# A mixture-of-experts layer: gathering tokens already transposed, in a fixed TensorE order, from weights stored tile by tile

## The chip, the core and the metric

The kernel runs on one core of one Trainium2 chip. The metric is the device time of one execution in microseconds (us). TensorE is called PE in the profile, its weight loads PEld, VectorE DVE, ScalarE ACT, GpSimd POOL and SyncE SP. SP issues nearly all transfers from HBM; its queue is written SPq.

## What is computed

One layer on 256 tokens of 2048 float32 features. Its first part is a token mixer (stick-breaking attention, a state-space layer, an mLSTM, three gated projections and an output projection), which reads most of the other float32 weights. Its second part, which most of this text is about, is a mixture of 32 experts:

```python
gates = (one_hot(g_idx, N_GROUPS)[:, :, None] * within[:, None, :]).reshape(-1, N_EXPERTS)
hid = silu(einsum('td,edf->tef', t, w1)) * einsum('td,edf->tef', t, w3)
y = einsum('tef,efd->td', hid * gates[:, :, None], w2)
```

Each token goes to one of 4 groups and there to 2 of 8 experts. An expert has `w1` and `w3` (2048 x 256 each) and `w2` (256 x 2048): 6 MiB, and 192 MiB (201.3 MB) for all 32. All are read once.

## The kernel before, in words

**The mixer.** Weight matrices are read in tiles of 512 rows by 512 columns (`load_raw`, DMA on L118) into a ring of three 1 MiB buffers. Each tile is split into a high and a low part (`split`: ACT cast on L131, DVE subtraction on L132), and three matmuls are made of it (L142 to L144). A tile is a 512-column piece of 512 rows, so its source runs are 2 KiB long. The conditioning matrix `w_ada` is read the same way: its first tiles by `ada_pe` (DMA L321, matmul L327) and `ada_first` (L295), in 2 KiB runs, the rest by `ada_rest` (L353 on DVE), in 4 KiB runs. Nothing of the mixer can start before the 8 MiB of `ada_pe` are there, as they give the modulation of the first input block.

**The router.** After the output projection a chain of small DVE operations finds for each token its experts and its place (rank) among the tokens of each expert pair. `keep_warm` matmuls fill PE meanwhile. In this part the order of PE, DVE and ACT is written out by hand (`manual_schedule`).

**The experts.** Experts are taken in 8 units of four; a unit is two half-groups of 64 tokens, and two `Pair` steps (`n`, with `el` = 0 and 1) of two experts each. A unit's tokens are gathered by matmul with a 0/1 selection (`sel_unit`, L1276). `Gather.rows` (L1312) has the selection as stationary operand and gives tokens on partitions; `scale` (L1317, ACT) multiplies by the norm; `turn` transposes on PE (L259, tile `xgT`) so that features are on partitions; `finish` modulates into `XG` (`modulate`, L1284 on ACT, L1287 on DVE). The transposes read every fourth column. The gather of unit u+1 is spread over the two pairs of unit u.

A `Pair` loads 12 tiles of 1 MiB (`load_in`, L1377: `w1` and `w3` for four row blocks and two experts, each tile as two DMAs of 512 KiB in 4 KiB runs; `load_out`, L1391: `w2`, four DMAs of 1 MiB in 8 KiB runs; in the very last pair L1388, 4 KiB runs). The tiles go round 11 buffers (`moe_raw`). `mm_in` multiplies `XG` by `w1` and `w3` (tile `h`), `hidden` applies the gated activation (ACT L1409, DVE L1410), `hidden_turn` transposes it (tile `hT`, copied on L1419), `mm_out` multiplies by `w2` (tile `y`). Both run on L1397, as two half-array matmuls, one per expert, at column positions 0 and 64:

```python
for h in range(2):
    sl = slice(64 * h, 64 * h + 64)
    nc.tensor.matmul(o[sl, :], lhsT=lhsT[:, sl], rhs=rhs(h), start=start, stop=stop,
                     tile_position=(0, 64 * h), skip_group_check=True)
```

At the end of a unit its four 512-column results are scaled and split (L1431, L1432, L1436), and in the next unit they are scattered back to the tokens by matmul and addition (`combine_mm`, tile `sc`, L1446; `combine_add`, L1455). Between router and last pair the order of the instructions on each engine is the framework's, not the program's. After the last pair come the final norm (L1722 to L1724) and the output (L1717).

Of the kernel before, what the change touches and what calls it, by code (L numbers as in the profile page):

```python
# [10 lines left out]
F32 = mybir.dt.float32  # L11
# [33 lines left out]
def kernel(ctx: ExitStack, tc: tile.TileContext, A, out, dbg=None):  # L45
# [44 lines left out]
    def cols4(v):  # L90
        return v.rearrange("(j p k) -> p j k", p=P, k=4)

    craw = cp.tile([P, 4, 4], F32, name="craw")
    nc.sync.dma_start(out=craw, in_=cols4(A["c"]))
    x_load()
    nc.gpsimd.dma_start(out=cst[:, :256], in_=A["consts"][:, :256])
    ball = cp.tile([P, 24, 4], F32, name="ball")
    nc.gpsimd.dma_start(out=ball[:, :8], in_=cols4(A["b_ada"])[:, :8])
    gmix = cp.tile([P, 4, 4], F32, name="gmix")
    nc.gpsimd.dma_start(out=gmix, in_=cols4(A["norm_mix_g"]))  # L100
    gmoe = cp.tile([P, 4, 4], F32, name="gmoe")
# [150 lines left out]
    def rows4(mat, c0):  # L252
        return lambda j: mat[512 * j:512 * j + 512, c0:c0 + 512].rearrange("(p k) c -> p k c", k=4)

    def rows_kp(mat, c0):
        return lambda j: mat[512 * j:512 * j + 512, c0:c0 + 512].rearrange("(k p) c -> p k c", p=P)
# [52 lines left out]
    def ada_pe(j):  # L309
# [6 lines left out]
        for jr in range(4):  # L316
            for kp in range(2):
                raw = pap.tile([P, 2, 2, 512], F32, tag="raw", bufs=3, name=f"ada{j}_{jr}_{kp}")
                for v in range(2):
                    c0 = v * D + 512 * j  # L320
                    nc.sync.dma_start(out=raw[:, v], in_=A["w_ada"][512 * jr:512 * jr + 512, c0:c0 + 512]  # L321
                                      .rearrange("(p k) c -> p k c", k=4)[:, 2 * kp:2 * kp + 2, :])
# [14 lines left out]
    def ada_rest():  # L337
        cols = []
        for v in (2, 3, 4, 5):
            for half in range(2):  # L340
                acc = pbp.tile([P, 1024], F32, tag="acc", bufs=1, name=f"accr{v}_{half}")
                for n in range(16):
                    jr, kp, q = n // 4, n // 2 % 2, n % 2
                    if q == 0:
                        c0 = v * D + 1024 * half
                        raw = load_raw(A["w_ada"][512 * jr:512 * jr + 512, c0:c0 + 1024]
                                       .rearrange("(p k) c -> p k c", k=4)[:, 2 * kp:2 * kp + 2, :],
                                       (2, 1024), f"adar{v}_{half}_{jr}_{kp}")
# [60 lines left out]
    def s5_params():  # L409
# [115 lines left out]
        nc.gpsimd.dma_start(out=br, in_=A["s5_b_re"].rearrange("(j g) p h -> (g p) j h", g=2))  # L525
        nc.gpsimd.dma_start(out=bi, in_=A["s5_b_im"].rearrange("(j g) p h -> (g p) j h", g=2))
# [42 lines left out]
        for r, nm in enumerate(("s5_c_re", "s5_c_im")):  # L569
            cc = cut(0, 8, 64)  # L570
            nc.gpsimd.dma_start(out=cc, in_=A[nm].rearrange("(u g) h p -> (g h) u p", g=8))
# [174 lines left out]
    def gates_chunk():  # L746
        wif = pap.tile([P, 2, 2, 512], F32, tag="raw", bufs=3, name="wif")[:, 0, 0, :128].rearrange("p (k c) -> p k c", k=16)
        for j in range(4):
            nc.gpsimd.dma_start(out=wif[:, 4 * j:4 * j + 4, :],
                                in_=A["w_in"][512 * j:512 * j + 512, COL["gates"]:COL["gates"] + 8]  # L750
                                .rearrange("(p k) c -> p k c", k=4))
# [199 lines left out]
    for j in range(4):  # L951
# [12 lines left out]
        if j == 2:  # L964
            nc.sync.dma_start(out=cst[:, 256:], in_=A["consts"][:, 256:])
            nc.sync.dma_start(out=ball[:, 8:], in_=cols4(A["b_ada"])[:, 8:])
            nc.sync.dma_start(out=gmoe, in_=cols4(A["norm_moe_g"]))
# [197 lines left out]
    wrg = pd.tile([P, 2, 16, 36], F32, tag="wrg", name="wrg")  # L1165
    wr, wg = wrg[:, 0], wrg[:, 1]
# [14 lines left out]
    L2 = pd.tile([P, 36], F32, name="L2")  # L1181
# [12 lines left out]
    L1 = pd.tile([P, 2, 36], F32, name="L1")  # L1194
# [22 lines left out]
    def out_copy(c4, tt, pt):  # L1217
        xt = pd.tile([P, 4, 128], F32, tag="x1T", bufs=2, name=f"x1Ts{c4}{tt}")
# [13 lines left out]
    def split_x1(tt, c4, part):  # L1232
        sl = slice(512 * c4, 512 * c4 + 512)
        if part == 0:
# [411 lines left out]
    for n in range(2 * NU - 1):  # L1646
# [24 lines left out]
        elif gat:  # L1671
            nxt.turn(2 * el)
# [108 lines left out]
```

## Time and profile before

| what | us |
|---|---|
| three runs of the kernel: lowest, median, highest | 1597.33, 1601.37, 1603.70 |
| the profiled execution, its own time | 1600.31 |
| its span in the trace | 1598.5 |
| PE busy | 1509.0 (94%) |
| DVE busy | 1015.1 (64%) |
| ACT busy | 568.6 (36%) |
| weights of the experts multiplied, first to last (PE) | about 1093 to 1580 |

Bytes moved: 488.13 MB, 201.3 MB of them weights of the experts. A row of the stretches view has, after the stretch and its length, the busy time and the number of instructions of PE, PEld, DVE, ACT and POOL, then the clock granted to PE (1.00 is 2.4 GHz), the mean busy share of the 16 DMA engines (overlapping packets can bring it a little over 1) and the GB/s that they moved. A row of the chain has start, length and what ran. In the groups view, a row gives line, engine, operation, tiles, shapes and count, then busy time and the mean of one in ns, then the idle time ahead of it.

### The profile page before, as it was taken

The numbers are of one execution on the slowest core, as the hardware profiler recorded it, in microseconds if no ns is written. First come the engines' busy times: TensorE is split into PE (matmuls) and PEld (weight loads), VectorE is DVE, ScalarE is ACT, GpSimd is POOL, SyncE is SP. The second block draws the span as 40 slices with busy tenths as digits, with TensorE's granted clock in tenths as the row PEclk, the third lists the DMA queues.
The fourth block names the chain that finished last, engine by engine and source line by source line (L and its number), as shares of the span: only waits on it lengthen the run. The fifth ranks groups of instructions, "written<-read, shape, count | busy, mean of one in ns | idle before, by whom it ended". The sixth has DMA issues, their size and how long they took to land.

```text
span 1598.5 us, 25021 instructions
## 1 busy us (share of the span) xinstructions
PE 1509.0 (94%) x10228; PEld 1140.2 (71%) x10228; DVE 1015.1 (64%) x1733; ACT 568.6 (36%) x755; POOL 39.0 (2%) x63
## 2 busy tenths in 40 slices
PE   4999999989999998999999999999999999999996
PEld 2999999888888988899999998874334433443332
DVE  0879997889879999999778866553213212222124
ACT  3554363774534333333444344342112111111112
POOL 1000010010000000000000010000000000000000
PEclk9999999999999999999999999999999999999998
DMA  9998967677787676777789976566999999999994
GB/s 343 386 348 305 319 191 222 220 223 261 247 300 265 229 264 231 273 264 264 263 308 327 318 267 241 207 228 257 414 413 412 413 402 374 412 392 411 404 412 183
DMA packets 172249, 488.13 MB, mean 305 GB/s; under 512 B 13876, under 2 KB 14048, under 8 KB 162784
## 3 DMA queue, kind: packets, MB, share of 16 engines
q1 hardware_dynamic: 168464, 473.27, 80.5%
q0 software_dynamic: 3088, 12.14, 2.3%
q8 instruction: 82, 1.34, 0.3%
q10 hardware_dynamic: 576, 1.05, 0.2%
q14 instruction: 39, 0.32, 0.1%
HBM read 479.06 MB, written 6.31 MB: 304 GB/s over the span
## 4 chain that ended last, share of the span: by engine, by line
PE 54%; DVE 25%; DMA 10%; issue 6%; ACT 4%; POOL 0%; SPq 0%; ACTq 0%; DVEq 0%; POOLq 0%
PE h L1397 14%; PE y L1397 9%; DVE accr L353 5%; DMA adar<-in_w_ada_dram 4%; DVE g_sb_w L132 2%; DVE g_ml_w L132 2%; PE sc L1446 2%; PE wo_b L143 2%; PE wo_b L144 2%; PE wo_b L142 2%; DVE bu L698 2%; PE xg L1312 2%; DVE s5pp L695 2%; DVE bu L697 1%; DVE s5qq L696 1%
## 5 line engine op out<-in xcount | busy, mean ns | idle before, releaser
L1397 PE MATMUL h<-w,XG 128*64 128x512 f32 x1024 | 245.3, 599 | 0.0
L1397 PEld LDWEIGHTS h<-w,XG 128*64 128x64 f32 x1024 | 75.7, 137 | 139.1 <-issue 137.4
L353 DVE SCALAR_TENSOR_TENSOR accr<-adar,ccol,accr 128x1024 f32<-128x1024 f32 x120 | 153.5, 1280 | 18.2 <-DMA adar<-in_w_ada_dram 17.3
L1397 PE MATMUL y<-w,hh 128*64 128x512 f32 x512 | 150.4, 598 | 0.5 <-ACT hh L1419 0.5
L1410 DVE SCALAR_TENSOR_TENSOR s<-h,gg,s 128x256 f32<-128x256 f32 x16 | 7.7, 484 | 167.8 <-ACT s L1409 167.8
L1455 DVE TENSOR_TENSOR x<-x,sc 128x512 f32<-128x512 f32 x64 | 43.0, 682 | 105.7 <-PE sc L1446 105.7
L1397 PEld LDWEIGHTS y<-w,hh 128*64 128x64 f32 x512 | 49.0, 136 | 81.5 <-issue 77.7
L1409 ACT ACTIVATE s<-h 128x256 f32<-128x256 f32 x16 | 6.1, 383 | 212.3 <-PE h L1397 212.3
L144 PE MATMUL g_sb_b<-hT,g_sb_w 128*128 128x256 f32 x256 | 73.1, 285 | 8.5 <-DVE g_sb_w L132 8.4
L144 PE MATMUL g_ml_b<-hT,g_ml_w 128*128 128x256 f32 x256 | 72.4, 283 | 3.3 <-DVE g_ml_w L132 3.3
L1287 DVE TENSOR_SCALAR XG<-xgT,G,modc 128x128 f32<-128x128 f32 x64 | 26.0, 410 | 77.0 <-ACT XG L1284 77.0
L144 PE MATMUL g_s_b<-hT,g_s_w 128*128 128x256 f32 x256 | 72.1, 282 | 1.6 <-DVE g_s_w L132 1.4
L142 PE MATMUL g_ml_b<-hT,g_ml_w 128*128 128x256 f32 x256 | 72.4, 283 | 0.0
L142 PE MATMUL g_sb_b<-hT,g_sb_w 128*128 128x256 f32 x256 | 71.9, 281 | 0.0
L142 PE MATMUL g_s_b<-hT,g_s_w 128*128 128x256 f32 x256 | 71.7, 280 | 0.0
L143 PE MATMUL g_s_b<-hT,g_s_w 128*128 128x256 f32 x256 | 71.6, 280 | 0.0
L143 PE MATMUL g_ml_b<-hT,g_ml_w 128*128 128x256 f32 x256 | 71.5, 279 | 0.0
L143 PE MATMUL g_sb_b<-hT,g_sb_w 128*128 128x256 f32 x256 | 71.4, 279 | 0.0
L132 DVE TENSOR_TENSOR wo_w<-wo_w,wo_w 128x1024 fp32r<-128x1024 f32 x32 | 39.0, 1223 | 31.8 <-ACT wo_w L131 31.6
L303 DVE SCALAR_TENSOR_TENSOR acc<-ada,ccol,acc 128x1024 f32<-128x1024 f32 x45 | 57.6, 1281 | 0.5
L131 ACT CAST g_ml_w<-g_ml_w 128x1024 fp32r<-128x1024 f32 x32 | 32.0, 1048 | 70.4 <-DMA g_ml_w<-in_w_in_dram 47.4
L144 PEld LDWEIGHTS g_sb_b<-hT,g_sb_w 128*128 128x128 f32 x256 | 48.1, 188 | 11.2 <-DVE g_sb_w L132 11.1
(506 smaller groups left out, 4361.7 us busy)
## 6 DMA issues: line engine op xcount, KB each, us to landing
w<-in_moe_w_dram SPq DMA_DIRECT2D x256, 512.0 KB, 9.2
adar<-in_w_ada_dram SPq DMA_DIRECT2D x64, 1024.0 KB, 5.5
w<-in_moe_w_dram SPq DMA_DIRECT2D x64, 1024.0 KB, 9.9
ada<-in_w_ada_dram SPq DMA_DIRECT2D x64, 512.0 KB, 7.5
g_sb_w<-in_w_in_dram SPq DMA_DIRECT2D x16, 1024.0 KB, 5.4
g_ml_w<-in_w_in_dram SPq DMA_DIRECT2D x16, 1024.0 KB, 5.4
g_s_w<-in_w_in_dram SPq DMA_DIRECT2D x16, 1024.0 KB, 6.1
wo_w<-in_w_out_dram SPq DMA_DIRECT2D x16, 1024.0 KB, 5.1
```

Of the source, the lines that this page charges most:

```text
L131: nc.scalar.copy(out=hv, in_=src)
L132: nc.vector.tensor_tensor(out=lv, in0=src, in1=hv.bitcast(F32), op=ALU.subtract)
L142: nc.tensor.matmul(o, lhsT=lhs[0], rhs=rhs[0], start=start, stop=False, **kw)
L143: nc.tensor.matmul(o, lhsT=lhs[0], rhs=rhs[1], start=False, stop=False, **kw)
L144: nc.tensor.matmul(o, lhsT=lhs[1], rhs=rhs[0], start=False, stop=stop, **kw)
L303: nc.vector.scalar_tensor_tensor(acc, raw[:, :, q], cs, acc, op0=ALU.mult, op1=ALU.add)
L353: nc.vector.scalar_tensor_tensor(acc, raw[:, q], cs, acc, op0=ALU.mult, op1=ALU.add)
L695: V.tensor_tensor(out=pp, in0=L2R, in1=prev, op=ALU.mult)
L698: V.tensor_tensor(out=cur, in0=cur, in1=qq, op=ALU.add)
L1312: nc.tensor.matmul(self.pt[j], lhsT=self.sel[:, tt], rhs=xs[i][:, tt, 512 * j:512 * j + 512], start=(i == 0 and tt == 0), stop=(i == 1 and ...
L1397: nc.tensor.matmul(o[sl, :], lhsT=lhsT[:, sl], rhs=rhs(h), start=start, stop=stop, tile_position=(0, 64 * h), skip_group_check=True)
L1455: V.tensor_tensor(out=x1[:, tt, sl], in0=x1[:, tt, sl], in1=pts[tt], op=ALU.add)
```

## The change

Two things are changed, in one kernel.

**Layout.** The weights reach the chip in another order, made by numpy ahead of the launch (`laid_out`): each tile that the kernel loads lies in one piece, 8 KiB per partition. `w1` and `w3` are one array, whose tile is one DMA of 1 MiB; so are the two halves of a `w_ada` tile. The eight gate columns of `w_in` and the small vectors are arrays of their own. `w2` keeps its layout.

**Gather.** `Gather` becomes `Batch`, for two units at once. Here the rows of the tokens (`xs`) are the stationary operand and the selection (256 columns) the moving one, so features come out on partitions and nothing is transposed. For that `split_x1` writes `xs` with its columns in block order. The norm is spread over partitions by a matmul (`norms`) and multiplied on DVE. `rank` gets 1000 taken off for members, so that one comparison on DVE gives the selection. Three `X` buffers go round. The gather of the first batch begins ahead of the first pair and goes on between its `mm_in` steps; the later ones lie in the pairs of odd units. In the loop over pairs the order of PE is written out by hand.

```diff
     def rows4(mat, c0):
-        return lambda j: mat[512 * j:512 * j + 512, c0:c0 + 512].rearrange("(p k) c -> p k c", k=4)
+        return lambda j: mat[(c0 - 8 * (c0 > 8192)) // 512, j].rearrange("p (k c) -> p k c", k=4)
...
-                for v in range(2):
-                    c0 = v * D + 512 * j
-                    nc.sync.dma_start(out=raw[:, v], in_=A["w_ada"][512 * jr:512 * jr + 512, c0:c0 + 512]
-                                      .rearrange("(p k) c -> p k c", k=4)[:, 2 * kp:2 * kp + 2, :])
+                nc.sync.dma_start(out=raw.rearrange("p v k c -> p (v k c)"), in_=A["w_ada"][8 * j + 2 * jr + kp])
...
     def split_x1(tt, c4, part):
         sl = slice(512 * c4, 512 * c4 + 512)
+        src = x1[:, tt, sl].rearrange("p (q k) -> p k q", k=4)
+        hi, lo = (x[:, tt, sl].rearrange("p (k q) -> p k q", k=4) for x in xs)
...
+    class Batch:
+        def __init__(self, b):
+            self.b = b
+            self.sel = pd.tile([P, 2, 256], F32R, tag="sel", bufs=2, name=f"sel{b}")
+            for tt in range(2):
+                V.tensor_tensor(out=self.sel[:, tt].rearrange("p (i s) -> p i s", i=4),
+                                in0=iotam[:, None, :].to_broadcast([P, 4, 64]),
+                                in1=rank[:, tt, 4 * b:4 * b + 4][:, :, None].to_broadcast([P, 4, 64]),
+                                op=ALU.is_equal)
...
         def norms(self):
+            pt = psum("ms", f"r2p{self.b}")
             for tt in range(2):
+                nc.tensor.matmul(pt[:, :256], lhsT=r2[:, tt:tt + 1].to_broadcast([P, 128]),
+                                 rhs=self.sel[:, tt].bitcast(F32), start=(tt == 0), stop=(tt == 1))
...
         def rows(self, j):
+            for half in range(2):
+                pt = psum("ms", f"xg{self.b}{j}{half}").rearrange("p (q s) -> p q s", q=2)
+                for q in range(2):
+                    kk = 2 * half + q
+                    for n in range(4):
+                        i, tt = divmod(n, 2)
+                        nc.tensor.matmul(pt[:, q, :], lhsT=xs[i][:, tt, 512 * j + 128 * kk:512 * j + 128 * kk + 128],
+                                         rhs=self.sel[:, tt], start=(n == 0), stop=(n == 3), skip_group_check=True)
+                self.pt[j, half] = pt
         def finish(self, j):
+            for half in range(2):
...
+                V.tensor_tensor(out=t, in0=self.pt.pop((j, half)), in1=self.r[:, None, :].to_broadcast([P, 2, 256]),
+                                op=ALU.mult)
+                for q in range(2):
+                    k = 4 * j + 2 * half + q
+                    nc.scalar.activation(self.units[0].X[:, k, :], t[:, q, :128], AF.Identity,
+                                         bias=modc[:, 3, k:k + 1], scale=G2[:, k:k + 1])
+                    V.tensor_scalar(self.units[1].X[:, k, :], t[:, q, 128:], G2[:, k:k + 1], modc[:, 3, k:k + 1],
+                                    op0=ALU.mult, op1=ALU.add)
...
-                raw = moe_raw(f"w13_{e}_{j}").rearrange("p (w k f) -> p w k f", w=2, k=4)
-                for wi, nm in enumerate(("moe_w1", "moe_w3")):
-                    nc.sync.dma_start(out=raw[:, wi], in_=A[nm][e, 512 * j:512 * j + 512, :]
-                                      .rearrange("(p k) f -> p k f", k=4))
-                self.raw[j].append(raw)
+                raw = moe_raw(f"w13_{e}_{j}")
+                nc.sync.dma_start(out=raw, in_=A["moe_w13"][e, j])
+                self.raw[j].append(raw.rearrange("p (w k f) -> p w k f", w=2, k=4))
...
+        ba = Batch(0)
+        ba.norms()
+        ba.rows(0)
+        ba.finish(0)
+        for tt in range(2):
+            split_x1(tt, 3, 1)
...
+        gat = u % 2 == 1 and u + 1 < NU
...
+        with tc.manual_schedule(engines={ENG.PE}):
+            cur.mm_in(0)
+            if n == 0:
+                ba.rows(1)
+                ba.finish(1)
+            cur.mm_in(1)
+            if n == 0:
+                ba.rows(2)
+                ba.finish(2)
+            if gat:
+                if el == 0:
+                    ba = Batch(u // 2 + 1)
+                    ba.norms()
+                ba.rows(2 * el)
+                ba.finish(2 * el)
+            cur.mm_in(2)
+            if gat:
+                ba.rows(2 * el + 1)
+                ba.finish(2 * el + 1)
+            if n == 0:
+                ba.rows(3)
+                ba.finish(3)
+                ga.gates()
+                ga.back()
+            cur.mm_in(3)
+            cur.hidden()
+            if done is not None:
+                combine_add(2 * el, combine_mm(done[0], done[1][el][:, 0], u - 1, 2 * el))
+            cur.hidden_turn()
             if el == 0:
+                py = [psum("mm", f"y{u}_{c}") for c in range(4)]
             for c in range(4):
+                cur.mm_out(0, c, py)
+            if done is not None:
+                combine_add(2 * el + 1, combine_mm(done[0], done[1][el][:, 1], u - 1, 2 * el + 1))
+            for c in range(4):
+                cur.mm_out(1, c, py)
...
+    def tiles(m, order):
+
+        m = m.reshape(m.shape[-2:])
+        r, c = m.shape[0] // 512, m.shape[1] // 512
+        if order == "pk":
+            t = m.reshape(r, P, 4, c, 512).transpose(3, 0, 1, 2, 4)
+        else:
+            t = m.reshape(r, 4, P, c, 512).transpose(3, 0, 2, 1, 4)
+        return t.reshape(c, r, P, 2048)
...
+    w13 = np.stack([z["moe_w1"].reshape(NE, 4, P, 4, FF), z["moe_w3"].reshape(NE, 4, P, 4, FF)], axis=3)
+    a["moe_w13"] = w13.reshape(NE, 4, P, 2048)
```

## Rows read from the trace of the kernel before

**Rows 1.** The page: PE's share, and DMA in the 40 slices.

```profile
PE 1509.0 (94%) x10228; PEld 1140.2 (71%) x10228; DVE 1015.1 (64%) x1733; ACT 568.6 (36%) x755; POOL 39.0 (2%) x63
...
DMA  9998967677787676777789976566999999999994
GB/s 343 386 348 305 319 191 222 220 223 261 247 300 265 229 264 231 273 264 264 263 308 327 318 267 241 207 228 257 414 413 412 413 402 374 412 392 411 404 412 183
```

**Rows 2.** Stretches: mixer, experts' loads of each kind, and steady state.

```profile
50.00:75.00 25.00, 25.00 (x191) 23.91 (x190) 20.28 (x18) 11.56 (x15) 0.00 (x0) 1.00 1.05 386
...
1136.00:1152.00 16.00, 15.65 (x77) 6.46 (x74) 8.46 (x20) 5.13 (x11) 0.00 (x0) 1.00 1.03 409
...
1126.00:1132.00 6.00, 6.00 (x28) 2.16 (x26) 0.00 (x0) 0.69 (x1) 0.00 (x0) 1.00 1.01 425
1156.00:1162.00 6.00, 6.00 (x30) 2.17 (x30) 1.28 (x2) 0.59 (x1) 0.00 (x0) 1.00 1.01 422
...
1184.00:1280.00 96.00, 92.38 (x389) 37.38 (x387) 26.31 (x57) 17.07 (x34) 0.00 (x0) 1.00 1.02 413
...
560.00:640.00 80.00, 71.65 (x586) 69.56 (x585) 78.19 (x187) 25.95 (x28) 0.00 (x0) 1.00 0.72 248
```

**Rows 3.** The chain in order of time, in the experts.

```profile
1114.13 7.07 PE y L1397 x32
...
1422.00 4.54 PE y L1397 x16
...
1440.27 10.50 PE h L1397 x48
...
1457.89 0.93 PE sc L1446 x4
...
1485.24 4.55 PE y L1397 x16
```

**Rows 4.** PE's waits in the first 100 us (total, times, longest).

```profile
PE adarp L327 <- DMA ada<-in_w_ada_dram: 18.4, 8, 12.0
```

**Rows 5.** Groups by line and form, 1296 to 1359.2 us.

```profile
L1312 PE MATMUL xg<-xs,sel 128*128 128x512 f32 x16 | 4.5, 413 | 0.3 <-DVE r2s L1306 0.3
L1284 ACT ACTIVATE XG<-xgT,modc,G 128x128 f32<-128x128 f32 x9 | 4.1, 457 | 9.9 <-PE xgT L259 7.7 <-DVE XG L1287 1.9
...
L259 PE MATMUL xgT<-cst,xgr 128*128 128x128 f32 x16 | 2.8, 296 | 0.0
...
L1431 DVE TENSOR_TENSOR yt<-y,gb 128x512 f32<-128x512 f32 x4 | 2.6, 685 | 1.4 <-PE y L1397 1.4
```

**Rows 6.** Instructions in order of time on PE: mixer, router, last pair.

```profile
131.00 0.28 PE L143 MATMUL sbq_b<-hT,sbq_w 128*128 128x256 f32 x1
131.12 0.28 PE L144 MATMUL sbq_b<-hT,sbq_w 128*128 128x256 f32 x1
...
1082.02 1.11 PE L1499 MATMUL warm<-cst 128*128 128x512 f32 x2
...
1093.02 4.56 PE L1397 MATMUL h<-w,XG 128*64 128x512 f32 x12
...
1571.36 5.37 PE L1397 MATMUL y<-w,hh 128*64 128x512 f32 x24 [0.52 <-ACT hh L1419]
```

**Rows 7.** SP's DMA issues, in order of time.

```profile
1098.40 0.33 SPq L1391 DMA_DIRECT2D w<-in_moe_w_dram  x1
```

**Rows 8.** Stretches at the end of the experts' loads.

```profile
1566.00:1568.00 2.00, 2.00 (x12) 0.62 (x10) 0.69 (x2) 0.00 (x0) 0.00 (x0) 1.00 0.99 395
1568.00:1570.00 2.00, 2.00 (x11) 0.81 (x8) 0.13 (x1) 0.38 (x1) 0.01 (x1) 1.00 0.29 119
```

**Rows 9.** Stretches with gaps on PE: before the mixer, after the router.

```profile
24.00:28.00 4.00, 2.68 (x40) 1.09 (x40) 0.00 (x0) 0.00 (x0) 0.00 (x0) 1.00 1.00 354
...
32.00:36.00 4.00, 2.70 (x40) 1.30 (x40) 2.23 (x2) 0.78 (x1) 0.00 (x0) 0.62 1.04 391
...
1090.00:1100.00 10.00, 8.86 (x40) 4.70 (x42) 4.21 (x22) 2.21 (x6) 0.00 (x0) 0.83 0.10 14
```

More of the change, by code (lines that the diff above doesn't have):

```diff
@@ L318, in ada_pe @@
                 raw = pap.tile([P, 2, 2, 512], F32, tag="raw", bufs=3, name=f"ada{j}_{jr}_{kp}")
[L319 to L322, printed above, removed]
+                nc.sync.dma_start(out=raw.rearrange("p v k c -> p (v k c)"), in_=A["w_ada"][8 * j + 2 * jr + kp])
                 for kk in range(2):
@@ L1255 @@
     NU = 8
+    AWAY = 1000.0
+    iotam = pd.tile([P, 64], F32, name="iotam")
+    V.tensor_scalar(iotam, iota[:, 0:64], -AWAY, None, op0=ALU.add)
     def sm(shape, nm, dt=F32):
@@ L1269, in first_max @@
         return mx, oh
-    def sel_unit(u):
-        sel = pd.tile([P, 2, 128], F32R, tag="sel", bufs=2, name=f"sel{u}")
-        for tt in range(2):
-            for h in range(2):
-                V.tensor_scalar(sel[:, tt, 64 * h:64 * h + 64], iota[:, 0:64], rank[:, tt, 2 * u + h:2 * u + h + 1],
-                                mem[:, tt, 2 * u + h:2 * u + h + 1].bitcast(F32), op0=ALU.is_equal, op1=ALU.mult)
-        return sel
     def modulate(pT, j, h):
@@ L1308, in rows @@
+            self.r = pd.tile([P, 256], F32, tag="r2s", name=f"r2s{self.b}")
+            V.tensor_copy(out=self.r, in_=pt[:, :256])
         def rows(self, j):
[L1309 to L1317 removed]
@@ L1319, in turn @@
-        def turn(self, j):
-            self.pT[j] = psum("ms", f"xgT{self.u}{j}").rearrange("p (k s) -> p k s", k=4)
-            x = self.x.pop(j)
-            for kk in range(4):
-                transpose(self.pT[j][:, kk, :], x[:, kk::4], P)
-        def finish(self, j):
-            modulate(self.pT.pop(j), j, self.X[:, 4 * j:4 * j + 4, :])
+            for half in range(2):
[7 more added lines that the diff above has]
+                self.pt[j, half] = pt
@@ L1328, in gates, with __init__, X @@
+    class Unit:
+        def __init__(self, u, sel):
+            self.u, self.sel = u, sel
+        @property
+        def X(self):
+            return XG[:, self.u % 3] if self.u % 3 < 2 else XG2
         def gates(self):
@@ L1464 @@
     w = wo.split(3)
[L1465 removed]
+    lg = part(2, 36)
     rank = sm([P, 2, 16], "rank_t")
@@ L1565 @@
         V.tensor_tensor(out=within, in0=oh1, in1=oh2, op=ALU.add)
-        ga.turn(2)
-        ga.scale(3)
-        ga.finish(2)
-        ga.turn(3)
-        ga.finish(3)
-    ga.gates()
-    ga.back()
+    XG2 = pd.tile([P, 16, P], F32, tag="XG2", name="XG2")
+    ga = ba.units[0]
     cnt_ps = psum("ms", "cnt")
@@ L1653 @@
             cur.load_out(f)
-        cur.mm_in(0)
-        cur.mm_in(1)
-        if gat:
-            if el == 0:
-                nxt = Gather(u + 1)
-                nxt.norms()
-                nxt.gates()
-            nxt.rows(2 * el)
-            nxt.scale(2 * el)
-        cur.mm_in(2)
-        if gat:
-            nxt.rows(2 * el + 1)
-            nxt.scale(2 * el + 1)
-        cur.mm_in(3)
-        cur.hidden()
-        if done is not None:
-            combine_add(2 * el, combine_mm(done[0], done[1][el][:, 0], u - 1, 2 * el))
-        elif gat:
-            nxt.turn(2 * el)
@@ L1673 @@
-        cur.hidden_turn()
-        if done is not None and gat:
-            nxt.turn(2 * el)
-        if gat:
-            nxt.finish(2 * el)
-        if el == 0:
-            py = [psum("mm", f"y{u}_{c}") for c in range(4)]
-        for c in range(4):
-            cur.mm_out(0, c, py)
-        if gat:
-            nxt.turn(2 * el + 1)
-            nxt.finish(2 * el + 1)
-        if done is not None:
-            combine_add(2 * el + 1, combine_mm(done[0], done[1][el][:, 1], u - 1, 2 * el + 1))
@@ L1770 @@
     arrays, args = {}, {}
[L1771 to L1772 removed]
+    for name, a in laid_out(inputs).items():
         arrays[f"in_{name}_dram"] = a
```

168 lines of the change are left out of this document (73 added, 95 removed).

## The prediction, made before the change was run

> **What bounds the kernel now.** I read the page first. PE is busy 94% of the span, but the DMA row says more: near 9 in the first two slices, 5 to 9 through the mixer, and a flat 9 at about 410 GB/s from slice 29 on [rows 1]. So the experts have two candidates, and the share of PE doesn't choose between them. The stretches view does: from 1184 to 1280 us PE is busy 92.4 of 96 us and DMA has a share of 1.02 at 413 GB/s [rows 2]. Both are full. The chain names PE: the same `y` comes round after 1485.24 - 1422.00 = 63.24 us [rows 3], one unit. A unit's weights are 24 MiB, 25.17 MB; in 63.24 us that asks for 398 GB/s, 4% under the 413 that the queue gives. PE holds the end, DMA stands right behind it. A change that only quickens PE could win little more than 4% of the stage; one that only quickens DMA, next to nothing of it. This change does both.
>
> In the mixer PE is full too, except in the first 40 us, where it waits 18.4 us for `w_ada` [rows 4], and between 480 and 720 us, where it waits on DVE, itself busy 78.2 of 80 us [rows 2].
>
> **What a run length is worth.** Three kinds of stretch have DMA full. With 2 KiB runs in the mixer it gives 386 GB/s, with `w1` and `w3` alone (4 KiB) 409, with `w2` alone (8 KiB) 425 and 422 [rows 2]. After the change nearly all weights have the layout of `w2`, so I take 422: a tile of 1 MiB (1.0486 MB) then needs 2.485 us. The lower bound is the mixture of now, 413 (2.54 us); the upper one 425 (2.47 us).
>
> By the Trainium skill, "DMA: Bandwidth & Descriptors", Specifications, a transfer reaches line rate from 512 B on; by that rule the layout would win nothing on the stream, and the sum would end at the third rival's 1579. The rows' 386, 409 and 422 speak against it.
>
> **PE's work per pair after the change.** `h`: three of four `mm_in` take 10.50 us [rows 3], so 14.0 us. `y`: 7.07 us for all 32 instructions in the first unit, where nothing is put between them, but 4.54 us for 16 later [rows 3]. I read the difference as the order: two halves run side by side only if the two column positions alternate, and a hand-written order makes them alternate. I take 7.07; the other bound is twice 4.54, 9.1. `sc`: two times 0.93, 1.9 us. Hidden chain and transpose of `h`, partly behind `sc`: about 1.5 us. Together 24.4 us.
>
> The gather before: 16 `xg` over 4.5 us and 16 `xgT` over 2.8 us [rows 5], about 7 us per unit. After: 64 matmuls of 256 columns per two units, 0.12 us apart as in the mixer [rows 6], 7.7 us; and `norms`, two float32 matmuls of 256 columns, by half of the 1.11 us that 512 columns took [rows 6] at most 0.55 each (bounds 0.4 and 0.55). With 0.45 each that is 8.6 us per two units. On DVE, `finish` adds eight multiplications of 512 columns per two units at 0.685 us [rows 5]; DVE and ACT have room, and I cost that at nothing while PE has slack. If it had none, a late product would hold the PSUM buffers of the next `rows` and with them PE.
>
> So a pair without a gather asks for 24.4 us of PE, one with half a batch 28.7, the mean is 26.5. The stream needs 12 x 2.485 = 29.8 us per pair. **PE falls behind the stream as the bound**: what is late next is the weights, and PE's further gain is lost waiting for them.
>
> **The start of the stage.** `rank` is ready just after 1082 us; the first `h` runs at 1093.02 [rows 6], after the whole gather. After the change it needs selection (two DVE operations, under 0.7 us each by [rows 5]), `norms` (1.0), half of `rows(0)` (0.95), the product (0.69) and one ACT piece (0.46), with hops about 1086.4. Then `mm_in(0)` to `mm_in(3)` with three `rows` between them (1.9 us each and about 0.6 of waiting for ACT) end at 1108. Buffers are freed in steps: the stream restarts at 1090 instead of 1098.4 [rows 7], but until about 1119 it runs with small gaps and brings 10 tiles; before, at 0.41 MB per us from 1098.4 on, 8 by then. `split_x1`'s strided copies and the 1000 in `rank` replace operations of the same size and stay off this path.
>
> **The end.** 192 tiles are loaded, 11 ahead of the loop, 10 by 1119, so 171 remain: 171 x 2.485 = 425 us, to 1544. Before, the stream ended at about 1568.6 (119 GB/s in the last two us of [rows 8]). The last pair's four `w2` tiles keep 4 KiB runs, worth 0.3 us. From the stream's end to the span's end 29.9 us passed before. Then `y` began its third 512 columns at about 1575, 16 of the 24 instructions after 1571.36 [rows 6], 6.4 us after the data. When the data are the bound, that slack goes and 23.5 us remain: 1567.5 in place of 1598.5, 31 us less.
>
> **The mixer.** Up to 40 us the core moves some 13 MB at 343 to 386 GB/s [rows 1]; at 422 that is 35 down to 31 us. The first input block waits for it, so I take 4 us (0 to 6). Later DMA time is hidden by PE or DVE: DVE's work in the 480 to 720 us is unchanged. I take 2 us for loads that a split waits for (0 to 8). The gate columns, the vectors and the small state-space weights lie behind this work on POOL's queue; nothing is taken for them. SP issues 8 instead of 16 transfers per pair for `w1` and `w3` and has time left in both kernels.
>
> **Sum.** 1600.31 (the profiled execution) - 31 - 4 - 2 = 1563.3. That execution is 1.1 us under the median of the runs shown, so against the median I predict 1564 us.
>
> **Rivals.**
>
> 1. PE stays the bound (0.08). If `y` keeps its 4.54 us, and the fixed order makes PE wait for DVE or ACT, say 1.5 us per unit, a unit falls from 63.24 by the gather's 2.6 only and gains 1.5: 62.1. Seven units win 8 us, the start 6.6, the mixer 6: 1580. For it: a hand-written order cannot fill a gap with other work. Against: 11 buffers hold nearly a pair of weights, so a late PE takes nothing from the stream unless it is late on average over units.
>
> 2. The clock falls, and it ends slower (0.05). With DMA the bound, PE pauses about 1.5 us after every 3.5. The granted clock stood at 0.62 from 32 to 36 us, while PE waited for `w_ada` in pieces, and at 0.83 from 1090 to 1100 [rows 9]. If a share s of the stage ran at 1.2 instead of 2.4 GHz, a pair's 26.5 us of PE work would take 26.5 / (1 - s/2). From s = 0.32 on a pair takes longer than the present 31.6; with s = 0.5 it takes 35.3, 15 pairs lose 56 us, start and mixer give 13 back: 1643. Against: from 24 to 28 us PE was busy 2.68 of 4 us, no more than from 32 to 36, and the clock stayed at 1.00 [rows 9]; the new pauses have the same share, so it alone does not bring the clock down. By the Trainium skill, "TensorE: Matmul & The Clock Gate", HAM oscillation, PE work shorter than the wait for the next weights restarts at the low clock each time. Here the work is the longer of the two.
>
> 3. The stream gets no faster (0.12). At 413 a tile stays at 2.54 us; 171 tiles end at 1553.5, the span at 1577, and the mixer wins nothing: 1579. For it: the shares of 1.01 to 1.05 in [rows 2] show engines full at each run length, so the differences could lie in what else they carried. Against: the order 386, 409, 422 holds.
>
> 4. More is won in the mixer (0.09): over 10 us beyond the 6, if waits that end at DVE there begin with DMA: 1552.
>
> 5. Nothing changes by more than 0.5%, about what a measurement of this kernel can tell from none (0.03): two of the above at once.
>
> **How the numbers follow.** The forecast has the remaining 0.63. Its own range, from the bounds on the tile (2.47 to 2.54: -3, +9), the mixer (0 to 14 against 6) and the start (3 either way), is about 1553 to 1578. To hold 8 in 10 it is drawn to the first and third rival and to most of the fourth: 1551 to 1586. Faster by over 0.5%: forecast and rivals 1, 3 and 4, 0.92. Within: 0.03. Slower: rival 2, 0.05.
>
> **What would show it.** DMA near 420 GB/s at a share of 1.0 from about 1110 to the stream's end; the period of a unit close to 59.6 us; `h` waiting for DMA in nearly every `mm_in`, at a granted clock of 1.00; no `xgT`; two `y` blocks of about 3.5 us each per pair; first `h` near 1082 (with the mixer's 4 to 6 us off). Wrong would be: dips in DMA while PE is full (rival 1), a low clock in steady state (rival 2), 410 GB/s with `h` waiting (rival 3).

## The result and the profile after

The changed kernel takes 1578.54 us (median of 4 runs, 1576.6 to 1579.05), the kernel before beside it 1602.53 (4 runs, 1597.33 to 1603.92): a ratio of 0.9855, with a 95% interval of 0.9834 to 0.9876. That is faster by 24 us, where 37 were forecast; 1578.5 lies in the range and 14 us from the number. The profiled execution took 1578.53 us, its span is 1576.8, against 1598.5 before.

The page after, PE's share and the DMA rows of the 40 slices, which answers to [rows 1]:

```profile
PE 1470.8 (93%) x10212; PEld 1133.0 (72%) x10212; DVE 1030.6 (65%) x1738; ACT 553.2 (35%) x723; POOL 32.4 (2%) x58
...
DMA  9988956567587667676789875647999999999994
GB/s 373 371 333 306 339 183 235 197 230 268 215 317 260 240 241 266 237 275 255 273 320 347 307 277 221 244 160 299 387 421 421 421 421 421 422 421 421 422 420 194
```

From slice 30 on the DMA rate is one number, 421 (420 to 422), where before it went between 374 and 413; the last slice is the end. PE's share hardly moved (94 to 93%), so it says nothing about which of the two is the bound.

Stretches after, which answer to [rows 2] (the mixer, the DVE-bound part, steady state) and, the first two, to [rows 9]. The columns are those of before: busy time of PE, PEld, DVE, ACT, POOL with counts, granted clock, DMA share, GB/s:

```profile
24.00:28.00 4.00, 2.93 (x50) 1.66 (x54) 0.00 (x0) 0.00 (x0) 0.00 (x0) 1.00 1.02 426
32.00:36.00 4.00, 3.47 (x60) 2.24 (x64) 0.98 (x1) 0.00 (x0) 0.00 (x0) 0.65 1.01 420
...
50.00:75.00 25.00, 25.00 (x193) 23.91 (x191) 20.09 (x17) 11.60 (x15) 0.00 (x0) 1.00 0.94 377
...
560.00:640.00 80.00, 71.78 (x582) 69.59 (x583) 78.24 (x187) 25.98 (x28) 0.00 (x0) 1.00 0.69 249
...
1184.00:1280.00 96.00, 89.22 (x406) 35.56 (x406) 30.23 (x59) 13.80 (x30) 0.00 (x0) 1.00 1.01 421
```

In steady state DMA's share is 1.01 (1.02 before), PE now has 7 of 96 us free, and the clock stays at 1.00 (2.4 GHz) through those pauses. From 50 to 75 us, where the old layout had DMA full at 386 GB/s, it now has a share of 0.94 with PE full: there the faster queue waits for PE. The stretch of 560 to 640 us is as before.

The chain in order of time in the experts, which answers to [rows 3]:

```profile
1300.10 19.81 DMA w<-in_moe_w_dram
...
1319.97 19.87 DMA w<-in_moe_w_dram
```

Where `y` and `h` stood there are transfers, each with its time from issue to landing. At 421 GB/s a tile of 1.0486 MB takes 2.49 us, so 19.87 us is the time of 8 tiles, which are in flight together, and a unit's 24 tiles take 59.8 us, against 63.24 before.

Groups after from 1300 to 1420 us (two units), answering to [rows 5]. Columns: busy us, mean ns, idle time before them:

```profile
L1399 PE MATMUL h<-w,XG 128*64 128x512 f32 x256 | 62.0, 598 | 7.3 <-DMA w<-in_moe_w_dram 7.3
L1399 PE MATMUL y<-w,hh 128*64 128x512 f32 x128 | 29.2, 598 | 2.1 <-ACT hh L1421 2.1
...
L1307 PE MATMUL xg<-sel,xs 128*128 128x256 f32 x62 | 8.4, 288 | 0.0
```

`h` waits for weights, in 7 of the 16 `mm_in` of these two units and for 1.4 us at most; `y` takes 14.6 us a unit, and `xgT` is gone. PE's waits for `ada` in the front, [rows 4], are 17.7 us where they were 18.4. PE in order of time at the router and in the last pair, which answers to [rows 6], then SP's restart, which answers to [rows 7]:

```profile
1082.69 2.26 PE L1307 MATMUL xg<-sel,xs 128*128 128x256 f32 x16
1084.88 0.25 PE L1566 MATMUL cnt<-mem,cst 128*1 128x16 f32 x4
1085.30 3.65 PE L1399 MATMUL h<-w,XG 128*64 128x512 f32 x16 [0.17 <-ACT XG L1319]
...
1545.81 4.50 PE L1399 MATMUL y<-w,hh 128*64 128x512 f32 x18 [0.52 <-ACT hh L1421]
1552.85 1.93 PE L1399 MATMUL y<-w,hh 128*64 128x512 f32 x6 [2.54 <-DMA w<-in_moe_w_dram]
```

```profile
1088.98 0.33 SPq L1393 DMA_DIRECT2D w<-in_moe_w_dram  x1
```

Last, the stretches of the ramp after the restart and of the stream's end, the latter answering to [rows 8]:

```profile
1090.00:1095.00 5.00, 4.22 (x25) 1.91 (x24) 2.50 (x6) 1.76 (x4) 0.00 (x0) 1.00 0.95 364
1095.00:1100.00 5.00, 4.57 (x30) 2.75 (x28) 2.50 (x6) 1.76 (x4) 0.00 (x0) 1.00 0.79 292
...
1110.00:1115.00 5.00, 5.00 (x25) 2.82 (x25) 0.00 (x0) 0.00 (x0) 0.00 (x0) 1.00 0.93 390
1115.00:1120.00 5.00, 5.00 (x26) 2.95 (x24) 0.00 (x0) 0.00 (x0) 0.00 (x0) 1.00 0.83 285
...
1550.00:1552.00 2.00, 0.31 (x1) 0.00 (x0) 0.80 (x2) 0.62 (x1) 0.00 (x0) 1.00 0.47 197
```

The same execution in marks: the router's `rank` matmul starts 1.05 us earlier than before (6 forecast), the first `h` 7.72 earlier, the stream ends at about 1550.9 (by the 197 GB/s of the last row) instead of 1568.6, and the span ends 21.7 earlier.

### The profile page after: what moved, and what is told of

It is laid out like the page before. It is cut to its first block, busy times and chain, and to the rows that moved or that the text cites. A ratio compares the mean times of both kernels' runs of the same rounds, so it can differ in the third digit from the quotient of the medians.

```text
span 1576.8 us, 24657 instructions
## 1 busy us (share of the span) xinstructions
PE 1470.8 (93%) x10212; PEld 1133.0 (72%) x10212; DVE 1030.6 (65%) x1738; ACT 553.2 (35%) x723; POOL 32.4 (2%) x58
## 3 DMA queue, kind: packets, MB, share of 16 engines
q10 hardware_dynamic: 576, 1.05, 0.2%
## 4 chain that ended last, share of the span: by engine, by line
PE 51%; DMA 23%; DVE 20%; ACT 3%; issue 2%; SPq 0%; DVEq 0%; ACTq 0%
DMA w<-in_moe_w_dram 19%; PE h L1399 6%; DVE accr L339 3%; PE y L1399 3%; DVE g_sb_w L126 2%; PE g_s_b L136 2%; PE wo_b L137 2%; PE g_s_b L137 2%; PE wo_b L138 2%; PE g_s_b L138 2%; PE wo_b L136 2%; DVE bu L684 2%; DVE g_ml_w L126 2%; PE xg L1307 2%; DVE s5pp L681 2%
## 5 line engine op out<-in xcount | busy, mean ns | idle before, releaser
L1399 PEld LDWEIGHTS h<-w,XG 128*64 128x64 f32 x1024 | 83.7, 136 | 165.3 <-issue 103.3
L339 DVE SCALAR_TENSOR_TENSOR accr<-adar,ccol,accr 128x1024 f32<-128x1024 f32 x120 | 153.6, 1280 | 16.7 <-DMA adar<-in_w_ada_dram 15.9
L1399 PE MATMUL y<-w,hh 128*64 128x512 f32 x512 | 117.9, 598 | 10.3 <-ACT hh L1421 7.7
L1399 PEld LDWEIGHTS y<-w,hh 128*64 128x64 f32 x512 | 35.8, 136 | 74.9 <-issue 59.8
L1319 ACT ACTIVATE XG<-xgr,modc,G 128x128 f32<-128x128 f32 x64 | 28.1, 486 | 125.7 <-DVE xgr L1315 125.6
L1315 DVE TENSOR_TENSOR xgr<-xg,r2s 128x512 f32<-128x512 f32 x32 | 22.0, 688 | 63.3 <-PE xg L1307 63.3
```

The lines of the kernel that those rows point to most:

```text
L339: nc.vector.scalar_tensor_tensor(acc, raw[:, q], cs, acc, op0=ALU.mult, op1=ALU.add)
```

## The experiments

The change has three separable parts: layout (L), gather (G) and the fixed order of PE (O). All their combinations were timed, each beside the kernel before on the same chip; the chips differ between rows, so rows are compared by their ratios. The intervals are 95% intervals.

| parts | ratio to before | interval | median us | unit in steady state |
|---|---|---|---|---|
| L | 0.9962 | 0.9946 to 0.9979 | 1594.54 | 63.23 |
| O | 0.9946 | 0.9931 to 0.9961 | 1589.94 | 60.8 |
| G | 0.9945 | 0.9927 to 0.9963 | 1588.61 | 59.7 |
| G + O | 0.9946 | 0.9916 to 0.9977 | 1591.38 | 60.9 |
| L + O | 0.9865 | 0.985 to 0.988 | 1577.59 | 59.8 |
| L + G | 0.985 | 0.982 to 0.988 | 1574.17 | 59.7 |
| L + G + O (the change, second time) | 0.9849 | 0.9831 to 0.9867 | 1574.82 | 59.8 |

The unit is the time from a `y` to the `y` of the next unit in the profiled execution, a mean over the middle units where they alternate. The parts don't add up: L wins 0.4% and O 0.5%, both together 1.35%, and G on top of both nothing that the intervals show.

**Layout alone.** The loads and the arrays of the change (the hunks on `rows4`, `w_ada`, `w_gates`, `vectors`, `load_in`), all else as before:

```diff
-                for wi, nm in enumerate(("moe_w1", "moe_w3")):
-                    nc.sync.dma_start(out=raw[:, wi], in_=A[nm][e, 512 * j:512 * j + 512, :]
-                                      .rearrange("(p k) f -> p k f", k=4))
+                nc.sync.dma_start(out=raw, in_=A["moe_w13"][e, j])
```

> The new layout alone, with the old gather and the framework's order on PE. Theory (before, PE held the experts and DMA stood right behind; the change takes 14 us off the stream and lets PE fall behind it, so neither part is worth much alone): a unit keeps PE's 63.2 us, DMA shows dips because its buffers are full, and only the front of the mixer wins about 1 us: 1599 to 1602 us. Rival (the stream was the bound all along, and the layout carries the gain): near the changed kernel, 1580 to 1586 us, a unit near 60 us.

Its groups over one unit, 1317.8 to 1381.03 us:

```profile
L1377 PE MATMUL h<-w,XG 128*64 128x512 f32 x128 | 30.5, 596 | 0.0
L1377 PE MATMUL y<-w,hh 128*64 128x512 f32 x65 | 20.6, 599 | 0.0
```

The unit is 63.23 us, for 63.24 before, and the mean DMA rate in it is 396 GB/s at a share of 0.96: a faster queue stands idle behind PE, as the theory said. The 1594.54 us are below its range of 1599 to 1602. In the profiled execution all of the gain lies ahead of the experts (the first `h` 8.27 us earlier, the last `y` 8.37), so it was larger than expected there and nil here.

**Gather and order, with the old layout.** The other hunks of the change.

> The new gather and the fixed order alone, from weights in the old order (w1 and w3 in two DMAs of 4 KiB runs). Theory: the stream becomes the bound at its old rate, 412 to 413 GB/s without a dip; a tile takes 2.54 instead of 2.49 us, 172 tiles 9 us more than in the changed kernel, and the mixer loses its 1 us: about 1588 us (1585 to 1591), PE waiting for weights in nearly every step. Rival (the gather and the order carry all of it, the run length means nothing): 1578 to 1580 us.

1591.4, just above the range of 1585 to 1591 and far from the rival's. DMA runs flat at 412 to 414 GB/s at a share of 1.02, `h` waits for it, and the unit is 24 x 2.54 = 60.9 us: the stream at its old rate.

**The change without the fixed order.**

```diff
-        with tc.manual_schedule(engines={ENG.PE}):
+        if True:
```

> The changed kernel without the hand-written order of PE in the loop over pairs; the framework orders it. Theory: y blocks go back from 3.6 to about 4.5 us, PE asks for up to 2 us more per pair (28.5 on the mean), still under the stream's 29.9: within 3 us of the changed kernel, DMA still at 421 GB/s. Rival (the fixed order is what wins): 1588 us or more, DMA with dips.

1574.2, a ratio of 0.985 where the changed kernel had 0.9855: the order is not what wins here. It is not without effect on PE, though; 100 us of steady state:

```profile
1200.00:1300.00 100.00, 96.98 (x426) 38.78 (x425) 31.34 (x62) 14.53 (x31) 0.00 (x0) 1.00 1.01 421
```

PE is 97% busy where the changed kernel needs 92, and `y` takes 18.2 us a unit for 14.6. From 1140 to 1540 us PE waits 13 us for DVE, ahead of `hT`, and 1.3 us for weights. So the unit of 59.7 us is PE's own, and it just fits into the stream's 59.8.

**Half the `w1` and `w3` transfers: PE's own pace after, and before.** In both kernels every second row block of `w1` and `w3` is multiplied with the tiles of the block ahead of it, so that a pair loads 8 tiles and not 12; the experts' result is then that of other weights. One run each:

```diff
+            if j % 2:
+                self.raw[j] = self.raw[j - 1]
+                return
```

> The changed kernel with half of w1 and w3 not loaded (the second and fourth row block use the tile of the block ahead), so the stream has 8 tiles per pair and cannot be the bound; PE's work is the same. Theory: PE's work per pair is what I summed, 24.4 us without and 28.7 with a gather, 26.5 on the mean: from the first h at 1085, 424 us, and 19 from the last y to the end: a span near 1528 us (1518 to 1540). Rival (PE's own work had been just under the stream's 29.9): 1555 us or more.

1533.67 us, span 1531.8; the unit is 54.1 us on the mean (59.0 with a gather in it, 49.1 without) at 98% PE and some 310 GB/s. So PE's need was forecast well (2 x 26.5 = 53.0).

> The kernel before, with every second w1 and w3 tile of the experts not loaded (the multiplications take the tile loaded just before it, so the routed result is that of other weights). Theory: before the change TensorE sets the experts' pace at 63.2 us per four blocks, transposes and waits for them included, so with half of those transfers gone the stage keeps its unit and the span stays within 4 us of 1598.5 but for the end and the start of the stage (1590 to 1600). Rival: the DMA stream already sets the pace before the change; then the stage shrinks as it did in the changed kernel with half the tiles, by over 30 us, to 1565 or less.

1548.07 us, span 1546.3: not what the theory said, and in the range that the rival gave. But the rival's cause isn't the one: with the layout alone the stream was faster and the unit stayed. Here the unit fell to 55.5 us with PE 100% busy at 305 GB/s. Two groups of the kernel before over one unit, 1296 to 1359.2 us, then those of this run over one unit, 1200.56 to 1256.10 us:

```profile
L1397 PE MATMUL y<-w,hh 128*64 128x512 f32 x65 | 20.6, 599 | 0.0
...
L259 PE MATMUL hT<-cst,s 128*128 128x128 f32 x4 | 0.9, 300 | 2.1 <-DVE s L1410 2.1
```

```profile
L1400 PE MATMUL h<-w,XG 128*64 128x512 f32 x130 | 29.4, 597 | 0.0
L1400 PE MATMUL y<-w,hh 128*64 128x512 f32 x64 | 14.6, 598 | 0.0
...
L259 PE MATMUL xgT<-cst,xgr 128*128 128x128 f32 x16 | 2.8, 296 | 0.0
L259 PE MATMUL hT<-cst,s 128*128 128x128 f32 x4 | 0.9, 301 | 0.0
```

Same instructions, transposes included, and PE is 7.7 us faster per unit. 6.0 of it is `y` (20.6 to 14.6), 1.1 `h`, and the 2.1 us of `hT` waiting for DVE are gone. The other groups nearly cancel. What differs is the order: the framework writes PE's order when the program is built, and with fewer loads it wrote another one. Before, of the four `y` blocks of a pair's first `w2` tiles, it puts three of one expert behind each other, then three of the other, and of the second tiles all four and all four; in the half kernel the experts alternate. This is the order in the built programs (w_21 and w_23 stand for the first tiles of the two experts):

```
before:  y_0<-w_21  y_1<-w_21  y_2<-w_21  y_0<-w_23  y_1<-w_23  y_2<-w_23  y_3<-w_21  y_3<-w_23
half:    y_0<-w_21  y_0<-w_23  y_1<-w_21  y_1<-w_23  y_2<-w_21  y_2<-w_23  y_3<-w_21  y_3<-w_23
```

The two experts' products are put on different column halves of the array (`tile_position`). What alternating may be worth can be read from PE in order of time in the kernel before, where the order happens to mix `y` and `h`:

```profile
1428.08 4.13 PE L1397 MATMUL y<-w,hh 128*64 128x512 f32 x13
1431.63 0.64 PE L1397 MATMUL h<-w,XG 128*64 128x512 f32 x1
1432.05 0.59 PE L1397 MATMUL y<-w,hh 128*64 128x512 f32 x1
1432.11 0.59 PE L1397 MATMUL h<-w,XG 128*64 128x512 f32 x1
```

Some starts lie 0.42 us apart (1431.63 to 1432.05), others 0.06 (1432.05 to 1432.11), where a matmul takes 0.59: two run side by side there. This made a theory that the run itself couldn't test, because it changed loads and order together: before the change it is PE's order, not the gather, that holds the unit at 63.2 us. The next run changes the order alone.

**The order alone.** The loop of the kernel before, wrapped:

```diff
+        with tc.manual_schedule(engines={ENG.PE}):
-        cur.mm_in(0)
+            cur.mm_in(0)
...
-            ga.back()
+                ga.back()
```

> The kernel before with the TensorE order of its loop over pairs written out by hand, in the order in which the program names the steps; old gather, old layout. Theory, formed after the run with half the transfers: before the change TensorE was full because its order sets several products of one column position behind each other (the y took 20.6 us of a unit, 14.6 in the half run), and that order alone held the unit at 63.2 us. Then the fixed order makes the stream the bound at 413 GB/s, 60.9 us per unit, 7 units win some 16 us: 1584 (1579 to 1590). Rival, the step of the prediction: the gather with its transposes fills TensorE; then within 4 us of the kernel before.

1589.94, at the edge of the expected range, and 9 us below the kernel before beside it (1599.18), so not the rival's. DMA is flat at 413 GB/s and PE no longer full, as two stretches of this kernel show:

```profile
1200.00:1300.00 100.00, 96.77 (x428) 39.86 (x424) 26.02 (x58) 17.52 (x34) 0.00 (x0) 1.00 1.02 413
1300.00:1400.00 100.00, 95.72 (x416) 40.12 (x416) 26.00 (x57) 18.55 (x36) 0.00 (x0) 1.00 1.02 413
```

```profile
L1397 PE MATMUL h<-w,XG 128*64 128x512 f32 x246 | 61.6, 598 | 5.6 <-DMA w<-in_moe_w_dram 5.6
L1397 PE MATMUL y<-w,hh 128*64 128x512 f32 x128 | 29.2, 599 | 0.0
```

These are its groups from 1300 to 1420 us: with every weight loaded and the order alone changed, two units' `y` take 29.2 us, 14.6 each, as in the half run, and `h` waits for weights. With old gather and all its transposes PE has time left. From the first `h` to the last `hT` the stage is 12.7 us shorter (464.85 for 477.55); 3.5 of that is lost again in the tail (31.4 for 27.9 us from the last `hT` to the span's end, 31.7 in the changed kernel), where, as in the changed kernel, the load of `final_g` now falls inside the stream (issued at 1555.89; before at 1569.99, behind it).

**Layout and order, old gather.**

> Layout and fixed order without the new gather. Theory: the unit is the stream's, 59.7 us at 421 GB/s, and only the earlier first h of the new gather is missing: 3.5 us for each of 7 units less than the layout alone (1594.5), about 1572 to 1580, next to the changed kernel. Rival: without the gather's saving TensorE stays the bound; then 1585 to 1593.

1577.59: the theory holds. Over 1300 to 1420 us, by its groups and then its chain:

```profile
L1377 PE MATMUL h<-w,XG 128*64 128x512 f32 x256 | 63.6, 598 | 3.7 <-DMA w<-in_moe_w_dram 3.7
L1377 PE MATMUL y<-w,hh 128*64 128x512 f32 x128 | 29.2, 598 | 0.0
...
L253 PE MATMUL xgT<-cst,xgr 128*128 128x128 f32 x32 | 5.6, 296 | 0.0
```

```profile
1310.90 19.81 DMA w<-in_moe_w_dram
...
1330.79 19.77 DMA w<-in_moe_w_dram
```

The transposes are all there and the pieces of the chain are those of the changed kernel. What the gather adds shows from `rank` to the span's end: 500.8 us here, 496.5 and 498.0 in the two profiles of the changed kernel, so some 3 to 4 of the 6.7 us by which it starts `h` earlier, and the intervals of the ratios don't separate even that.

**The gather alone.**

> The new gather alone: old layout, no fixed order. Theory: with the gather's saving TensorE is off the bound in either order, as with the layout; within 3 us of the run of gather and order (1591.4). Rival: the order matters without the layout; then 1595 or more.

1588.61, as with the order (ratio 0.9945 for 0.9946). In free order the new gather brings PE's unit from 63.2 to 59.7. That is below the old stream's 60.9 (DMA 413 to 414 at a share of 1.02), and the kernel can hold it for a while because it starts with tiles in hand and uses them up: up to 1480 us no `h` waits for weights, behind that they do, 8.2 us in six waits up to 1560. So TensorE is off the bound only late, not throughout as the theory had it. Nor is the 59.7 the gather's work alone, as two units of this run show, from 1300 to 1420 us:

```profile
L1419 PE MATMUL y<-w,hh 128*64 128x512 f32 x128 | 36.3, 598 | 0.0
```

`y` takes 18.2 us a unit, not 20.6: with another gather in it the framework wrote another order of `y` too. Of the gather's own products a unit has 4.7 us (9.3 in these two units), where `xg` and `xgT` took 7.3. How the 3.5 us divide between the gather and the order that came with it wasn't tried.

**The change a second time.**

> The changed kernel a second time, unaltered. Theory: the part of the layer ahead of the experts, which is the same code and gained 1 us where 6 were forecast, varies by several us from one profiled execution to the next, with how soon the TensorE clock comes back between 40 and 48 us. Then the first h starts 2 to 5 us ahead of its 1085.3 in the first profile, and the rest keeps its distances to it. Rival: the mixer gains 1 us from the layout and no more; then the first h starts within 1 us of 1085.3. Median by either within 4 us of 1578.5.

First `h` at 1082.55, 2.75 us earlier, and a median of 1574.82: the theory holds for the front. The rest didn't keep its distance: the span's end is only 1.15 us earlier, since the tail behind the last `hT` is 33.4 us for 31.7. In the front, 2.8 us appear between the first `u_b` (0.39 earlier) and the first `sbq_b` (3.19 earlier). The first rows are the second profile's, then come the first one's:

```profile
40.00:44.00 4.00, 3.69 (x31) 3.69 (x32) 4.00 (x7) 2.49 (x4) 0.00 (x0) 1.00 1.01 424
44.00:48.00 4.00, 4.00 (x37) 4.00 (x35) 3.96 (x4) 2.10 (x2) 0.00 (x0) 1.00 1.01 422
```

```profile
40.00:44.00 4.00, 3.30 (x15) 3.30 (x16) 4.00 (x7) 2.62 (x4) 0.00 (x0) 0.51 1.01 422
44.00:48.00 4.00, 4.00 (x25) 4.00 (x24) 3.96 (x5) 1.30 (x2) 0.00 (x0) 0.64 1.02 426
```

At a granted clock of 0.51 (nearly all at 1.2 GHz) and 0.64 (both levels mixed) PE does 40 matmuls in 8 us, at 1.00 it does 68. In both profiles PE had just waited 17.6 or 17.7 us in all for `ada` and 1.7 us for `hT`, and the clock had been low from 32 to 36 us (0.57 in the second profile, 0.65 in the first); in the first it fell again after 0.92 from 36 to 40 us, in the second it did not after 1.00.

**`final_g` behind the stream.**

```diff
-    nc.gpsimd.dma_start(out=fg, in_=A["final_g"]...
+    nc.sync.dma_start(out=fg, in_=A["final_g"]...
```

> The changed kernel with the load of final_g (1 MB) put on the queue of the weights, behind the last weight tile, as it fell in the kernel before. Theory: inside the stream it costs its bytes, 1 MB at 421 GB/s or 2.5 us; behind the stream it is hidden beside the last y and the combination. 1 to 3 us less than the changed kernel in this call. Rival: behind the stream it comes late for the final norm; then no gain, or up to 5 us more.

1571.83, 3.0 us less than the changed kernel's 1574.82; the four runs of each don't overlap (1570.38 to 1573.43 and 1573.46 to 1577.38). The ratio to before is 0.9836 (0.9817 to 0.9855). In the changed kernel POOL issues the load inside the stream; here it comes last, and the last pair's `y` no longer waits (24 in one piece, against 18, a wait of 2.54 us, and 6):

```profile
1544.43 0.54 POOL L1693 DMA_DIRECT2D fg<-in_final_g_dram  x1 [472.20 <-DMA w<-in_moe_w_dram]
```

```profile
1540.69 6.52 PE L1399 MATMUL y<-w,hh 128*64 128x512 f32 x24 [0.52 <-ACT hh L1421]
```

**Two more tiles ahead of the loop.**

```diff
-        n = ring_n[0] % 11
+        n = ring_n[0] - 2
...
+        if n < 0:
+            return pd.tile([P, 2048], F32, tag=f"Y{n + 2}", name=name)
+        n %= 11
```

> As the run before, and the first two w1/w3 tiles of the experts go into two of the four buffers of the accumulated output, which are idle until the first y, so that 13 tiles and not 11 are loaded ahead of the router. Theory: the DMA engines idle from about 1085 to 1089 for want of buffers, and the stage is bound by the stream; two tiles fewer in it are 2 x 2.49 us, so 4 to 5 us less, with final_g 6 to 8 us less than the changed kernel in this call, about 1571. Rival: the start of the stage is bound by TensorE; then the two tiles bring under 2 us beyond the run before.

1571.21 (ratio 0.9829, 0.9812 to 0.9846), 0.6 less than without them: the rival holds. (The theory's 1571 is met only because the changed kernel ran at 1574.8 this time; the step itself was to be 4 to 5 us.) The stretch 1090 to 1095 us, first here, then without the two tiles:

```profile
1090.00:1095.00 5.00, 4.57 (x28) 2.59 (x26) 2.01 (x5) 1.00 (x3) 0.00 (x0) 1.00 0.43 149
```

```profile
1090.00:1095.00 5.00, 4.57 (x30) 2.75 (x28) 2.50 (x6) 1.76 (x4) 0.00 (x0) 1.00 0.76 272
```

The first buffers that PE frees are now the two that aren't loaded again, so the stream restarts later (1091.7 for 1084.0). From 1085 to 1120 us it moves 9.8 MB (9.4 tiles), against 12.0 (11.4): 13 + 9.4 and 11 + 11.4 are the same 22.4 tiles by 1120, though this run's first `h` is 1.2 us later, worth half a tile. In the ramp PE sets how many tiles come, not the buffers.

**Without the fixed order, `final_g` behind the stream.** The edits of two runs above together.

> Gather and layout without the fixed order, with final_g behind the last weights. Theory: 2 to 4 us less than the same without that step (ratio to the kernel before 0.985), so a ratio of about 0.983, as the changed kernel with that step had. Rival: final_g does not matter where the order is free: 0.985.

1568.3 us, ratio 0.982 (0.9807 to 0.9833): the theory holds, and from `rank` to the span's end it is 492.7 us for 495.6 without that step, 2.9 less. Its ratio is the lowest of the study, but its interval overlaps those of the kernels with `final_g` moved and the order kept, and the changed kernel's second one; it lies just below the changed kernel's first (0.9834 to 0.9876).

## Why the prediction was right, and where its size was off

**What held.** PE and DMA were nearly tied before, so each of the edits alone was worth little and the two kinds together more: one kind alone wins 0.4 to 0.55%, layout with either of the other two 1.35 to 1.5%. Each kernel's unit is about the larger of two numbers. PE's is 63.2 us (old gather, free order), 59.7 (new gather, free order), 55.5 (old gather, alternating order, by the half run) or 54.1 (new gather, fixed order, likewise); the stream's is 60.9 at 413 GB/s or 59.8 at 421. The one exception is the gather alone, which lives on tiles in hand. The forecast had 53.0 for PE and 59.6 for the stream. The `y` of 3.5 us per 16 (measured 3.65), the first `h` 6.6 us sooner after `rank` (6.67) and the restart at 1090 (1089) came out as worked out. `h` was to wait for weights in nearly every `mm_in`; it does in 7 of 16, and the stream is the bound all the same.

**What was luck.** The forecast's own range ended at 1578, just short of the measured 1578.5; the stated range holds it because it was drawn to 1586 for rivals 1 and 3, and neither came true. (The bounds that it names make 1549 to 1581 when they are simply added up, so the 1553 to 1578 were too narrow as well.)

**Which part did it.** The prediction credited the gather and the order together with freeing PE. The runs show that either is enough. For the order they show why: of the 63.2 us of PE per unit it was worth 7, the transposes 2.8. For the gather they show it only together with the order of `y` that came along with it. The text read the difference between 7.07 and 4.54 us in [rows 3] as the order, but took it as one cost among others, and its upper bound of 9.1 us per pair was under what `y` took before (20.6 / 2 = 10.3).

**What was mis-sized.** In the profiled execution 21.7 us were won of 37; the missing 15 are terms of the sum, estimated from the marks of this trace:

- The mixer: 1.05 us of 6, so 5 us. Part of it is this execution: over nine profiles with the new layout `rank` starts at 1076.3 on average (1071.95 to 1080.31), over five with the old one at 1080.9 (1078.48 to 1082.73), so 4.6 us earlier on average, close to the 6. The first profile has the latest of the nine, and against the second 2.8 us of it are the low clock at 40 to 48 us. That is not all of the spread: two of the others (layout alone; `final_g` in free order) also had 0.57 from 40 to 44 us and yet the earliest `rank`; what else varies behind 400 us stays open. Of the 4 us for the first input block only 1.9 came on average (the first `u_b` at 38.2 for 40.1 us): in the first profile the queue runs at 418 to 426 GB/s from 24 to 40 us, but has gaps from 16 to 24 us (305 and 365 GB/s at shares of 0.87 and 0.98; before 387 and 344).
- The ramp: 9.1 tiles by 1119 where 10 were put, although `rank` is 1 us earlier here: some 3 us. The run with two more tiles shows that PE holds it.
- The stream's rate: 421 for 422 over 171 tiles, 1 us.
- `final_g` and the tail: its 1 MB was behind the stream before and is inside it now, 2.5 us at 421 GB/s, and the last `y` waits for what it delayed; the prediction had no term for it. The tail, from the stream's end to the span's, is 25.9 us where 23.5 were put. Together 4.9 us. Moving the load won 3.0 of them. The rest is the tail's own: from the landing of the last weight tile to the span's end there are 24.0 us in the changed kernel and still 23.5 with the load moved (28.6 before), so some 5 us of slack went where 6.4 were put.
- About 1 us is left without a name.

**The rivals.** The first (PE stays the bound, 1580) and the third (the stream no faster, 1579) gave a number nearer to the measured one than the forecast did, and both are wrong: PE waits 7.3 us for weights in two units, and the stream runs at 421 where the old layout gives 413 under the same bound (the run of gather and order). What makes the difference was not tried by itself, but the last pair's four `w2` tiles help: they have 4 KiB runs in DMAs of 1 MiB, the size of all other `w2`. In the kernel before they are the load of this stretch:

```profile
1562.00:1566.00 4.00, 4.00 (x16) 1.58 (x15) 0.60 (x1) 0.00 (x0) 0.00 (x0) 1.00 1.03 411
```

With the same size of DMA it is 411 GB/s here and 425 and 422 for the other `w2` [rows 2]; in the run with `final_g` moved it is 408 from 1534 to 1538 us, after 423. That speaks for the run length and against the size of the DMAs. So the rule of the Trainium skill, "DMA: Bandwidth & Descriptors", Specifications, that line rate is reached from 512 B on, is not what this case shows for runs of 4 and 8 KiB.

The second rival (the clock) fell as well: 1.00 from 1184 to 1280 and from 1300 to 1420 us, through pauses of up to 1.4 us. The fourth, more in the mixer, did not occur: its greatest gain in a profile is 9.4 us (`rank`, layout alone), where over 16 were meant.

## What to carry to other kernels

When two resources are within a few per cent of each other, time the parts of a change in combinations: single parts look worthless, and a part that looks like the heart of it (here the new gather) may be one of two ways to the same place. Where half-array matmuls should run side by side, look at the order in which they are issued, since a scheduler may group them, and write it out by hand before loads are taken away to see PE's own pace: here taking loads away changed the order as well. And when a stream ends earlier, list the small loads that used to come behind it.

## What was not expected of the hardware

The same 64 half-array matmuls of a unit took 20.6 or 14.6 us, with nothing changed but PE's order, in which the two column positions alternate or come in groups. In the free order of the new gather they took 18.2. The mean time of one is 598 or 599 ns in all three, so the mean hides it; the starts, 0.06 against 0.42 us apart, show it.

The same program in two profiles had a granted clock of 0.51 and 1.00 at 40 to 44 us after nearly the same waits, worth 2.8 us to everything behind it. What decides it was not tried.
